# Moving the first output products and the value quarters in the attention stage of a decoder trunk

## The chip, the cores and the metric

The kernel runs on one core of a Trainium2 chip. The metric is the device time of one execution in microseconds, the median of several runs. Engines are named as in the profile: PE is TensorE (matmuls), PEld its weight loads, DVE is VectorE, ACT is ScalarE, POOL is GpSimd, SP is the engine that issues the DMAs.

## What is computed

A trunk of two layers on 512 tokens of width 1024: a layer with a pooling mixer and a layer with stick-breaking attention (16 heads of 64), each followed by a squared-ReLU MLP of width 4096, with RMSNorms before and after each part. The change lies in the attention layer. Its core, cut from the reference:

```python
for i in range(S // Q_BLOCK):
    kv_len = (i + 1) * Q_BLOCK
    ...
    z = jnp.einsum('bhqd,bhkd->bhqk', q_blk, k_blk) * inv_sqrt_d
    mask = s_idx < t_idx
    log1m = jnp.where(mask, -jax.nn.softplus(z), 0.0)
    excl = lax.cumsum(log1m, axis=3, reverse=True) - log1m
    a = jnp.where(mask, jnp.exp(jax.nn.log_sigmoid(z) + excl), 0.0)
    outs.append(jnp.einsum('bhqk,bhkd->bhqd', a, v_blk))
...
q = jnp.matmul(h, w_q[j])
k, v = jnp.split(jnp.matmul(rms_norm(x, kv_norm_g), w_kv), 2, -1)
m = jnp.matmul(o, w_o[j])
```

## The kernel before

All matmuls run at high precision: each operand is split into a rounded part ("hi") and the remainder ("lo"), and a product is three matmuls, hi·hi, hi·lo, lo·hi (`mm3`, and `up_block` for the projections). The split of a weight is a copy on ACT (line 170) and a subtraction on DVE (line 172). Most attention weights are split during the MLP of layer 0, where `split_apart` takes them from the list `apart` and writes both parts to DRAM (`kept`); in the attention stage they come back by two DMAs each (line 243). Two are not in that list, o0 and o1, the first two blocks of the output projection: they are loaded raw (line 160) and split when their turn comes.

The attention stage works on eight pairs of heads. TensorE's order is written out in `ATT_ORDER` and is kept as written (`manual_schedule`); the orders of ACT, DVE and SP within the stage are found by the scheduler, with constraints such as `issue_after`. A word of the list is a letter, a pair (or a group of values) and its parts:

- `H`, `N`: the values of the first 8 heads, in halves, with the last norms of layer 0 between them.
- `P` k and q projections of a pair (48 matmuls, lines 719 to 723), `K` the first part of a k projection, `J` its rest, `Q` the q projection alone. Each result is split by ACT and DVE (lines 966 and 967).
- `S` scores of a pair (`scores`, line 1082, six PSUM banks), followed on ACT and DVE by sigmoids (1005, 1017), the scan (1021) and the product that gives the weights (1027), for two heads.
- `T` transposes of a pair's weights (`turn`, line 1040, six banks, 20 matmuls), copied out as `ah` by ACT (1046) and `al` by DVE (1050).
- `A` attention products of a pair (line 1057), copied out by ACT and DVE (1064, 1068) and split (292, 293) into a tile `ohl`, of which there are five.
- `V2s`, `V3s`: quarter s (128 tokens) of the values of heads 8 to 11 and 12 to 15 (24 matmuls of 256 columns, lines 311 to 313), written to one of two value tiles by ACT and DVE (898, 899). `V2` is used by pairs 4 and 5, `V3` by pairs 6 and 7. The first two value tiles are in the same two buffers, and serve pairs 0, 1 and 2, 3.
- `O0`, with two blocks of tokens at a time: the output products of pairs 0 and 1 (`out_proj`, `contract`; 24 matmuls of 512 columns), copied to `y` by ACT (line 456).
- `E`: `end()`, which does pair 7's scores and all other output products in `END_ORDER`.

PSUM has eight tiles, taken in turn (line 112). Weights are asked for in the order of their first use (`want`, lines 262 to 277), and loaded ahead by `fill`, up to four at a time, which runs after each projection, each `S`, and each block of tokens in `contract`. They take four buffers in turn (three `w`, one `wx`, `place`), so each waits for the release of the weight four places earlier. A raw weight needs one of the two `raw` buffers besides. `weight` puts the ACT and DVE halves of a split behind the latest such instructions at the time of the `fill` (`behind`).

The list of weights to be split in the MLP is the list of attention weights in their order of use, without o0 and o1, with the two parts v02, v03 moved behind q1 (lines 278 to 282).

Of the kernel before, what the change touches and what calls it, by code (L numbers as in the profile page):

```python
# [57 lines left out]

ATT_ORDER = [
    (w[0], int(w[1]), [int(c) for c in w[2:]])  # L60
    for w in """H001 N2 H101 N3 H023 H123 P0 K12 S0 P1 T0 K23 S1 J2 A0 Q2 T1 K33 S2 J3 A1 Q3 O001 T2 O023 S3 A2 P4 V20 T3 V21
    S4 A3 P5 V22 T4 V23 S5 A4 P6 V30 T5 V31 S6 A5 V323 P7 T6 E1""".split()
]

# [35 lines left out]
def trunk(ctx, tc, x, consts, grow, pw, wup, wdn, wq, wk, wv, wo, out):  # L106
# [68 lines left out]
    def gains(lo, n):  # L175


        def scaled(raw):
            m = max(n, 4)
            for k in range(m):  # L180
                c, at = raw[:, k * D // m : (k + 1) * D // m], lo + k * n // m
                nc.scalar.mul(c, c, gc[:, at : at + 1])  # L182

        return scaled

    gate, queue, made, ahead, dn_pool, att_pool, dn_raw = [False], [], {}, 4, [None], [None], {}

    def want(key, src, scaled=None):
        queue.append((key, src, scaled))
# [16 lines left out]
    apart, kept, going = [], {}, []  # L206
# [52 lines left out]
    for l in range(2):  # L259
        if l == 1:  # L260
            n = len(queue)
            for what, i, part in ATT_ORDER:
                if what == "H" and not i and 0 in part:
                    for h in range(4):
                        want(("v", 0, h), wv[h], gains(C_KV * KC + 2 * h, 2))
                elif what == "V" and 0 in part:
                    for h in range(2):
                        want(("v", i, h), wv[2 * i + h], gains(C_KV * KC + 4 * h, 4))
                elif what == "K":
                    want(("k", i), wk[i], gains(C_KV * KC, KC))  # L270
                elif what in "PQ":
                    if ("k", i) not in [k for k, _, _ in queue]:
                        want(("k", i), wk[i], gains(C_KV * KC, KC))
                    want(("q", i), wq[i], gains(C_MIX_PRE1 * KC, KC))
                elif what == "O" and 0 in part or what == "E":
                    for c in range(2 * i, 2 * i + 2 if what == "O" else PAIRS):
                        want(("o", c), wo[c])
            apart.extend(x for x in queue[n:] if x[0] not in [("o", c) for c in range(2)])
            at = [k for k, _, _ in apart].index(("v", 0, 2))
            later = [apart.pop(at) for _ in range(2)]  # L280
            at = [k for k, _, _ in apart].index(("q", 1)) + 1
            apart[at:at] = later

            queue[n - GRP : n + GRP] = queue[n : n + GRP] + queue[n - GRP : n]
        for j in range(NJ):
            want(("up", l, j), wup[l, j])
        for j in range(NJ - GRP, NJ):
            want(("dn", l, j), wdn[l, j])
# [442 lines left out]
    with tc.tile_pool(name="mix0", bufs=1, reuse_waits="tile") as mp:  # L731
# [12 lines left out]
        at = P + 4 * KC  # L744
# [145 lines left out]
    with tc.tile_pool(name="att", bufs=1, reuse_waits="tile") as ap:  # L890
# [82 lines left out]
        with tc.issue_after(latest["pool"].ins):  # L973
            nc.gpsimd.memset(begin, 0.0)
            for lo, n in SEG.values():
                c = min(n - P, 1)
# [371 lines left out]
```

## Time and profile before

| | |
|---|---|
| median of 3 runs | 948.79 us (948.14 to 948.91) |
| the profiled execution | 948.49 us, of which the span of the trace is 946.7 us |
| granted TensorE clock, mean | 0.999 |
| attention stage, first scores to the first of pair 7's | 403.9 to 561.4 us of the span |

Times of rows are microseconds from the start of the span. A row of the timeline gives the start, the length from the first start to the last end of a merged group, engine, line, operation, output and inputs (the program's names, without their numbers), sizes, and the count; behind it in brackets the idle time of the engine before it and what ended that. A row of the waits gives who waited for whom, the total in us, how often, and the longest. Ends of matmuls are modelled and neighbours overlap, so steps are measured from start to start.

### The profile page before, as it was taken

How to read it: one execution, taken by the hardware profiler on the slowest of the kernel's cores; microseconds unless marked ns; L12 is line 12 of the kernel's file. 1: busy time of each engine (PE TensorE's matmuls, PEld its weight loads, DVE VectorE, ACT ScalarE, POOL GpSimd, SP SyncE). 2: the span in 40 equal slices, each digit the busy share in tenths (PEclk: the TensorE clock that was granted, in tenths of full speed). 3: DMA queues.
4: the chain of work that ended last, by engine and by line, in shares of the span. 5: the costliest groups of instructions: out<-in, count | busy, mean ns of one | idle time of the engine just before them, and what ended most of it. 6: DMA issues, size and time to landing. Idle time of an engine off the chain costs nothing.

```text
span 946.7 us, 12348 instructions
## 1 busy us (share of the span) xinstructions
PE 937.5 (99%) x4701; PEld 789.6 (83%) x4702; DVE 696.2 (74%) x797; ACT 560.0 (59%) x983; POOL 41.1 (4%) x83
## 2 busy tenths in 40 slices
PE   9999999999999999999999999999999999999996
PEld 7998888888888888888888988898888888888885
DVE  5875798988978976278466668884696966958756
ACT  6667979888775647166544444875545444444532
POOL 2300000000000004000000001200000000000002
PEclk9999999999999999999999999999999999999999
DMA  8344969789697860631335271442514233133102
GB/s 312 95 178 144 345 219 347 291 282 356 218 323 266 293 203 2 222 134 45 136 109 179 98 259 45 136 154 82 184 45 142 81 133 111 45 134 112 39 6 90
DMA packets 43262, 156.15 MB, mean 165 GB/s; under 512 B 4289, under 2 KB 4673, under 8 KB 43202
## 3 DMA queue, kind: packets, MB, share of 16 engines
q1 hardware_dynamic: 43202, 155.36, 46.5%
q8 instruction: 37, 0.61, 0.3%
q14 instruction: 23, 0.19, 0.1%
HBM read 121.79 MB, written 33.55 MB: 164 GB/s over the span
## 4 chain that ended last, share of the span: by engine, by line
PE 95%; DVE 2%; ACT 1%; POOL 1%; issue 1%; POOLq 0%; DVEq 0%; ACTq 0%
PE ps L600 28%; PE ps L722 15%; PE ps L719 15%; PE ps L723 15%; PE ps L312 4%; PE ps L311 4%; PE ps L313 4%; PE ps L1057 2%; PE ps L1082 2%; PE ps L1040 2%; PE ps L840 1%; PE ps L406 1%; PE ps L812 1%; PE ps L767 1%; ACT xn L296 1%
## 5 line engine op out<-in xcount | busy, mean ns | idle before, releaser
L600 PE MATMUL ps<-w,a 128*128 128x512 f32 x1176 | 278.6, 389 | 0.0
L722 PE MATMUL ps<-xnh,w 128*128 128x512 f32 (+1 forms) x704 | 260.5, 372 | 0.0
L723 PE MATMUL ps<-xnl,w 128*128 128x512 f32 (+1 forms) x704 | 259.8, 370 | 0.0
L719 PE MATMUL ps<-xnh,w 128*128 128x512 f32 (+1 forms) x704 | 259.2, 370 | 0.1
L600 PEld LDWEIGHTS ps<-w,a 128*128 128x128 f32 x1176 | 220.7, 188 | 45.9 <-DVE w L293 0.2
L719 PEld LDWEIGHTS ps<-xnh,w 128*128 128x128 f32 x704 | 132.1, 188 | 22.9 <-DVE w L861 0.3
L723 PEld LDWEIGHTS ps<-xnl,w 128*128 128x128 f32 x704 | 132.7, 188 | 22.1
L722 PEld LDWEIGHTS ps<-xnh,w 128*128 128x128 f32 x704 | 132.3, 188 | 22.4
L609 DVE TENSOR_TENSOR y<-ps,y 128x512 f32<-128x512 f32 x124 | 84.2, 685 | 43.6 <-PE ps L600 43.5
L172 DVE TENSOR_TENSOR w<-raw,w 128x1024 fp32r<-128x1024 f32 x58 | 70.8, 1221 | 57.8 <-ACT w L170 57.6
L170 ACT CAST w<-raw 128x1024 fp32r<-128x1024 f32 x58 | 61.1, 1053 | 80.6 <-PE ps L719 80.6
L292 ACT CAST a<-r 128x768 fp32r<-128x768 f32 (+1 forms) x60 | 47.6, 794 | 71.9 <-PE ps L600 55.4
L293 DVE TENSOR_TENSOR a<-r,a 128x768 fp32r<-128x768 f32 (+1 forms) x60 | 54.0, 900 | 11.7 <-ACT a L292 11.6
L1021 DVE TENSOR_TENSOR_SCAN e<-u,begin 128x1280 f32<-128x1280 f32 x16 | 45.2, 2825 | 19.8 <-ACT u L1005 19.0
L292 ACT CAST w<-e 128x1536 fp32r<-128x1536 f32 (+1 forms) x30 | 41.9, 1395 | 22.8 <-DVE e L574 13.4
L293 DVE TENSOR_TENSOR w<-e,w 128x1536 fp32r<-128x1536 f32 (+1 forms) x30 | 49.4, 1646 | 1.8 <-ACT w L292 1.6
L182 ACT ACTIVATE apart<-apart,eye 128x128 f32<-128x128 f32 (+1 forms) x132 | 43.1, 406 | 0.7 <-DMA apart<-in_wk 0.7
L293 DVE TENSOR_TENSOR w<-w,w 128x1536 fp32r<-128x1536 f32 (+1 forms) x20 | 33.0, 1649 | 8.2 <-ACT w L292 8.2
L632 ACT ACTIVATE r<-ps 128x512 f32<-128x512 f32 x56 | 33.0, 589 | 8.9 <-PE ps L719 8.9
L293 DVE TENSOR_TENSOR w<-xn,w 128x1536 fp32r<-128x1536 f32 (+1 forms) x20 | 33.0, 1650 | 5.6 <-ACT w L292 5.5
L633 ACT ACTIVATE r<-r 128x512 f32<-128x512 f32 x56 | 35.5, 633 | 1.3
L296 ACT ACTIVATE xn<-y 128x512 f32<-128x512 f32 (+1 forms) x25 | 15.3, 613 | 31.6 <-DVE y L478 27.9
(134 smaller groups left out, 1331.2 us busy)
## 6 DMA issues: line engine op xcount, KB each, us to landing
raw<-in_wup SPq DMA_DIRECT2D x64, 512.0 KB, 4.1
w<-kept SPq DMA_DIRECT2D x60, 512.0 KB, 4.3
kept<-wx SPq DMA_DIRECT2D x30, 512.0 KB, 4.5
w<-in_wdn SPq DMA_DIRECT2D x8, 1536.0 KB, 6.7
kept<-apart SPq DMA_DIRECT2D x24, 512.0 KB, 6.0
xn<-in_wdn SPq DMA_DIRECT2D x8, 1536.0 KB, 7.8
apart<-in_wk SPq DMA_DIRECT2D x7, 512.0 KB, 7.4
apart<-in_wq SPq DMA_DIRECT2D x7, 512.0 KB, 9.1
```

Source lines behind the costliest of these rows:

```text
L170: nc.scalar.copy(hi, raw)
L172: nc.vector.tensor_tensor(out=lo, in0=raw, in1=hi.bitcast(F32), op=ALU.subtract)
L182: nc.scalar.mul(c, c, gc[:, at : at + 1])
L292: latest["act"] = nc.scalar.copy(hi, src)
L293: latest["dve"] = nc.vector.tensor_tensor(out=lo, in0=src, in1=hi.bitcast(F32), op=ALU.subtract)
L311: nc.tensor.matmul(dst, ah, bh, start=start, stop=False)
L600: nc.tensor.matmul(bank, a[:, x, q, TS[t]], w[:, z, q], start=start and q == 0 and k == 0, stop=q == self.n - 1 and k == 2, skip_group_che ...
L609: nc.vector.tensor_tensor(out=part, in0=bank, in1=part, op=ALU.add)
L719: nc.tensor.matmul(pu[:, cols], wl[:, k, :], xnh[:, k, cols], start=False, stop=k == KC - 1)
L722: nc.tensor.matmul(pu[:, cols], wh[:, k, :], xnh[:, k, cols], start=k == 0, stop=False)
L723: nc.tensor.matmul(pu[:, cols], wh[:, k, :], xnl[:, k, cols], start=False, stop=False)
L1021: nc.vector.tensor_tensor_scan(out=self.e[:, ::-1], data0=self.u[:, 1:][:, ::-1], data1=begin[:, ::-1], initial=0.0, op0=ALU.mult, op1=ALU ...
```

## The change

TensorE's order from pair 3's q projection on. `O001` and `O023` move from around the transposes of pair 2 to around those of pair 5, behind pair 6's projections; the quarters of the values take the places in front: `V20`, `V21` around pair 2's transposes, `V22`, `V23` around pair 3's, `V30`, `V31` around pair 4's, and `V323` between pair 4's attention products and pair 6's projections. The order in which weights are asked for follows: v20 and v21 now stand before k4, v30 and v31 before k6, o0 and o1 between q6 and k7. The list of weights to be split is written out as `SPLIT_ORDER` instead of being derived from the order of use; the sequence it lists is the one that the lines removed from it gave in the kernel before.

```diff
 ATT_ORDER = [
     (w[0], int(w[1]), [int(c) for c in w[2:]])
-    for w in """H001 N2 H101 N3 H023 H123 P0 K12 S0 P1 T0 K23 S1 J2 A0 Q2 T1 K33 S2 J3 A1 Q3 O001 T2 O023 S3 A2 P4 V20 T3 V21
-    S4 A3 P5 V22 T4 V23 S5 A4 P6 V30 T5 V31 S6 A5 V323 P7 T6 E1""".split()
+    for w in """H001 N2 H101 N3 H023 H123 P0 K12 S0 P1 T0 K23 S1 J2 A0 Q2 T1 K33 S2 J3 A1 Q3 V20 T2 V21 S3 A2 P4 V22 T3
+    V23 S4 A3 P5 V30 T4 V31 S5 A4 V323 P6 O001 T5 O023 S6 A5 P7 T6 E1""".split()
 ]
...
+SPLIT_ORDER = """v00 v01 k0 q0 k1 q1 v02 v03 k2 q2 k3 q3 k4 q4 v20 v21 k5 q5 k6 q6 v30 v31 k7 q7
+    o2 o3 o4 o5 o6 o7""".split()
...
-            apart.extend(x for x in queue[n:] if x[0] not in [("o", c) for c in range(2)])
-            at = [k for k, _, _ in apart].index(("v", 0, 2))
-            later = [apart.pop(at) for _ in range(2)]
-            at = [k for k, _, _ in apart].index(("q", 1)) + 1
-            apart[at:at] = later
+            asked = {x[0]: x for x in queue[n:]}
+            for what in SPLIT_ORDER:
+                key = (what[0], *(int(c) for c in what[1:]))
+                apart.append(asked.pop(key))
+            assert sorted(asked) == [("o", 0), ("o", 1)]
```

## The prediction

> **What bounds the kernel now.** I read the page first, for the engine that sets the end; then the waits of TensorE; then the timeline of TensorE, ScalarE and VectorE over the attention stage, the only stage whose order changes.
>
> ```profile
> span 946.7 us, 12348 instructions
> PE 937.5 (99%) x4701; PEld 789.6 (83%) x4702; DVE 696.2 (74%) x797; ACT 560.0 (59%) x983; POOL 41.1 (4%) x83
> PE 95%; DVE 2%; ACT 1%; POOL 1%; issue 1%; POOLq 0%; DVEq 0%; ACTq 0%
> ```
>
> TensorE is busy 99% of the span and is 95% of the chain that ended last. The change adds and removes no matmul, so it can gain only where TensorE stands still, and lose only by making it stand still somewhere new. The longest of its waits from 390 to 600 us, which hold the attention stage, is this (us in total, times, longest):
>
> ```profile
> PE ps L1082 <- DVE al L1050: 0.4, 2, 0.2
> ```
>
> It is a scores step (line 1082) that waits for VectorE to empty the transposes' banks (line 1050). The timeline shows which one; the scores of pair 1 come first, then those of pair 2.
>
> ```profile
> 420.02 0.53 PE L1082 MATMUL ps<-kh,qh 64*128 64x512 f32 x2
> 421.34 0.32 PE L1082 MATMUL ps<-kh,qh 64*128 64x256 f32 x2
> 422.11 0.50 PE L722 MATMUL ps<-xnh,w 128*128 128x512 f32 x1
> ...
> 438.04 0.49 PE L1082 MATMUL ps<-kh,qh 64*128 64x512 f32 x1
> 440.85 0.38 PE L1082 MATMUL ps<-kh,qh 64*128 64x256 f32 x1 [0.22 <-DVE al L1050]
> 441.69 0.50 PE L722 MATMUL ps<-xnh,w 128*128 128x512 f32 x1
> ```
>
> From the first matmul of the scores to the first of the next projection pair 1 takes 422.11 - 420.02 = 2.09 us, pair 2 441.69 - 438.04 = 3.65 us. The same 24 matmuls lose 1.56 us there. That is the one stall in this stage worth a tenth of a per cent.
>
> **Why it stalls.** There are eight banks. Scores take six, the transposes before them six, and one block of the next keys lies between. So the second bank of the scores waits for VectorE's first `al` of these transposes, and the last two, at 440.85, for its fourth and fifth. VectorE and ScalarE around the transposes of pair 0 (first row of each block) and of pair 1 (the others):
>
> ```profile
> 417.08 3.13 DVE L1050 TENSOR_TENSOR al<-ps,ah 128x512 fp32r<-128x512 f32 x6
> ...
> 430.10 1.20 DVE L172 TENSOR_TENSOR w<-raw,w 128x1024 fp32r<-128x1024 f32 x1
> 435.90 0.69 DVE L967 TENSOR_TENSOR ql<-ps,qh 128x512 fp32r<-128x512 f32 x1
> 436.85 1.23 DVE L172 TENSOR_TENSOR w<-raw,w 128x1024 fp32r<-128x1024 f32 x1 [0.26 <-ACT w L170]
> 437.99 2.21 DVE L1050 TENSOR_TENSOR al<-ps,ah 128x512 fp32r<-128x512 f32 x4
> ```
>
> ```profile
> 416.33 2.62 ACT L1046 CAST ah<-ps 128x512 fp32r<-128x512 f32 x6
> ...
> 435.28 0.58 ACT L966 CAST qh<-ps 128x512 fp32r<-128x512 f32 x1
> 435.76 1.05 ACT L170 CAST w<-raw 128x1024 fp32r<-128x1024 f32 x1
> 436.71 2.60 ACT L1046 CAST ah<-ps 128x512 fp32r<-128x512 f32 x6
> ```
>
> The rows of lines 170 and 172 are the splits of the two output weights o0 and o1, the only ones of this stage that come raw and are split here. That of o1 stands between the queries' split and `ah`/`al`, on both engines.
>
> **What the change removes there.** The output products move behind pair 6's projections, and o0 and o1 with them; v20 and v21 take their places in the ring of weights and come already split, by DMA alone. Without o1, `ah` starts at 435.76. In the pair 0 rows `al` follows `ah` by 417.08 - 416.33 = 0.75 us, so `al` starts near 436.51 (the `ql` before it is through by then, at 435.90 plus about 0.6), 1.48 us earlier. The last banks of the scores came free 440.85 - 437.99 = 2.86 us after `al` began, so now at 439.37. Undisturbed they are wanted 421.34 - 420.02 = 1.32 us after the start, at 439.36. So o1 alone takes the stall away to within a hundredth or so; that o0's 1.20 us at 430.10 goes too moves the work ahead of it up by about another microsecond, and is the spare. Bounds for the gain: 1.56 us, the whole stall, and 0.4 us, what the waits view adds up. I take 1.56.
>
> The two differ because the view counts idle time between a matmul's end and the next start, and I count from start to start. The page "Perfetto Trace Analysis" of the Trainium skill, section "Tensor Engine Instruction (MATMUL, LD_WEIGHTS)", says that the profiler computes a matmul's end from its size and does not observe it. By that rule the starts are the measurement and the sum is 1.56; by the view's rows it would be 0.4. The trace agrees with the rule: the next projection is late by all of the 1.56 us.
>
> **What it moves, and the cover left.** The same steps stand in another order, and the kinds of neighbours stay: an output half or a value quarter on either side of the transposes.
>
> ```profile
> 453.25 0.40 PE L311 MATMUL ps<-w,ohl 128*128 128x512 f32 x1
> 458.95 1.25 PE L1040 MATMUL ps<-eye,w 128*128 128x128 f32 x10
> 461.05 0.48 PE L311 MATMUL ps<-w,ohl 128*128 128x512 f32 x1
> 466.83 0.50 PE L1082 MATMUL ps<-kh,qh 64*128 64x512 f32 x2
> ...
> 482.46 0.28 PE L311 MATMUL ps<-w,xnh 128*128 128x256 f32 x1
> 485.33 2.35 PE L1040 MATMUL ps<-eye,w 128*128 128x128 f32 x20
> 490.47 0.50 PE L1082 MATMUL ps<-kh,qh 64*128 64x512 f32 x2
> ...
> 537.76 0.50 PE L1082 MATMUL ps<-kh,qh 64*128 64x512 f32 x2
> 542.43 0.34 PE L311 MATMUL ps<-w,xnh 128*128 128x256 f32 x1
> 548.24 0.40 PE L722 MATMUL ps<-xnh,w 128*128 128x512 f32 x1
> 559.15 1.04 PE L1040 MATMUL ps<-eye,w 128*128 128x128 f32 x8
> ```
>
> The first half of the output products takes 458.95 - 453.25 = 5.70 us, the second 5.78, transposes 2.10, a quarter of values 2.87, two quarters 548.24 - 542.43 = 5.81, scores with the attention products after them 542.43 - 537.76 = 4.67, a pair's projections 10.91. Two places lose cover between scores and transposes, where ScalarE and VectorE make the weights of two heads:
>
> ```profile
> 501.94 1.49 DVE L1027 TENSOR_TENSOR w<-w,e 128x1280 f32<-128x1280 f32 x1
> ```
>
> From the scores of pair 4 at 490.47 to the end of this, the last product of its weights, are 12.96 us. Pair 2's transposes stood at 458.95; with a quarter for a half, and the stall gone, they stand at 458.95 - 5.70 + 2.87 - 1.56 = 454.56, which is 16.5 us after its scores: 3.5 us to spare. Pair 6 loses the two quarters: from 559.15 - 537.76 = 21.4 us to 15.6, which leaves 2.6. If that cover failed, every microsecond that VectorE is late would be one on TensorE. Cost of both: nothing. After pair 2's transposes only a quarter stands before the scores, as at 490.47 for pair 4, which shows no wait.
>
> The value weights v20, v21 now stand where o0, o1 did, as four loads instead of two: their buffers (those of k2 and q2) come free before the scores of pair 2 at 438.04, and the first quarter stands at 454.56 - 2.87 = 451.7. The keys and queries of pair 5 now come into the value weights' buffers, as pair 6's did, behind the same steps and with the same 4.67 us:
>
> ```profile
> 512.79 2.23 SPq L243 DMA_DIRECT2D w<-kept  x4
> ...
> 518.78 0.45 PE L722 MATMUL ps<-xnh,w 128*128 128x512 f32 x1
> ```
>
> They were issued from 512.79 for a projection that starts at 518.78, and no wait shows. The same loads one pair earlier cost nothing again. So does the load of the gain row, now behind o2's on SP's queue, which waits for the end of the second output half near 542 us: its first use comes after pair 7's scores, over 20 us later. The values of pairs 4 to 7 overwrite buffers that pairs 0 to 3 have read by then (A1 and A3 stand ahead of V20 and V30).
>
> The splits of o0 and o1 go to a place with room. Counted back from the transposes of pair 6 at 559.15 - 1.56 = 557.59: its projections' partner P7 starts at 546.7, S6 at 542.0, the second output half at 536.2, T5 at 534.1, the first half at 528.4, P6 at 517.5. The buffers of o0 and o1 (those of v30, v31) come free at 517.5; o1 is queued behind the split of k6, whose product ends at about 523.0, so it is ready by 523.0 + 0.2 + 0.58 (that split) + 1.05 + 1.23 = 526.1, and wanted at 528.4. They hide under P6. Bounds: 0 and, if they slip behind the queries' split too (5.5 us later), 531.6 - 528.4 = 3.2 us. I take 0, as nothing holds them.
>
> **Sum.** 948.49 us for the profiled execution, less 1.56, is 946.93; this execution lay 0.30 under the median of 948.79, so the median comes to 947.23. Forecast 947.2.
>
> **Rivals.** (a) *The splits come too late.* This is the way to slower. For: o1's raw load is asked for next to k7's and q7's, and SP issues in order; if it is put behind q7's, whose buffer P6 holds until 528.4, it lands late.
>
> ```profile
> 343.68 5.30 SPq L160 DMA_DIRECT2D raw<-in_wo  x2
> DMA to landing us min/median/max: 3.5/4.1/4.3
> ```
>
> Issued at 528.8, landed at 532.9, split at 535.2: TensorE stands still for about 6 us from 529, less 1.56 gained, and the time is near 953.2. It decides once the raw load is issued later than about 524.3 (529.1 + 1.56 - 2.28 - 4.1). Against: both raw loads went out at 343.68, some 80 us before their splits, since nothing but the raw buffers holds them, and that stays so. The granted clock is whole in all 40 slices, so no row shows what a stop does to it:
>
> ```profile
> PEclk9999999999999999999999999999999999999999
> ```
> The page "TensorE: Matmul & The Clock Gate", section "Part 1: The HAM clock gate", says that an idle window of about 3.4 us halves the clock until another busy one; by it this case would cost up to 1.7 us more, an estimate from that page.
>
> (b) *Only the waits view's 0.4 us comes back*, because the planner puts other work in o1's place or the scores are held by something else: 948.4. For: the view's own sum. Against: no row between `qh` and `ah` but o1's.
>
> (c) *The later small waits go too*: with the value quarters gone from behind pair 6's scores, VectorE enters the end earlier.
>
> ```profile
> 560.02 0.69 DVE L967 TENSOR_TENSOR ql<-ps,qh 128x512 fp32r<-128x512 f32 x1 [4.75 <-ACT qh L966]
> 561.42 0.45 PE L1082 MATMUL ps<-kh,qh 64*128 64x384 f32 x2
> 563.72 0.49 PE L1057 MATMUL ps<-ah,v 128*128 128x512 f32 x1
> 592.55 1.27 PE L406 MATMUL ps<-eye,xn 128*128 128x128 f32 x8 [0.16 <-ACT xn L396]
> ```
>
> Pair 6's transposes last 2.27 us (559.15 to 561.42) against 2.10, pair 7's scores 2.30 against 2.09, and the wait at 592.55 is 0.16: together 0.5, so 946.7, and 946.0 if as much again lies hidden between starts. Against: VectorE already idles for 4.75 us before that `ql`, so it enters the end no earlier.
>
> **How the numbers follow.** Forecast 0.60, (a) 0.13, (b) 0.10, (c) 0.17. The forecast's own range is 946.7 to 947.7; the range reaches over (c) and (b), 946.0 to 949.0, and leaves out most of (a). A change under 0.2%, 1.9 us, can hardly be told from none in this kernel, whose three runs spread over 0.77 us. The forecast's 0.16% lies close under that bound: I give a quarter or so of it, and all of (c), to faster by over 0.2%: 0.17 + 0.15, rounded up to 0.33; (a) is slower, 0.13; the rest, 0.54, is within 0.2%.
>
> **What would show it.** In the profile after: the scores of pair 2 near 2.1 us long and no wait for line 1050; line 172 in the attention stage near 518 to 526 us, not 430 and 437; transposes of pairs 2 and 6 without a wait before them; scores of pair 7 at 559.9. A wait of TensorE at the first output half, or before pair 6's transposes, would make the forecast wrong, as would splits that still stand between `qh` and `ah`.

## The result, and the profile after

The changed kernel takes 947.25 us (median of 20 runs, 946.57 to 947.83), the kernel before 948.64 us in the 20 runs beside it: a ratio of 0.9985, 95% interval 0.9978 to 0.9992. The forecast was 947.2 us. The profiled execution took 947.41 us, its span 945.6.

The profile's page of the changed kernel: TensorE as busy as before, and the chain that ended last now hardly leaves it (97% after 95%, VectorE 1% after 2%).

```profile
span 945.6 us, 12346 instructions
PE 936.8 (99%) x4702; PEld 789.7 (84%) x4702; DVE 696.3 (74%) x797; ACT 560.0 (59%) x983; POOL 41.1 (4%) x83
PE 97%; POOL 1%; ACT 1%; DVE 1%; issue 0%; POOLq 0%; DVEq 0%; ACTq 0%
```

All waits of TensorE in it (us in total, times, longest). The changed file has six lines more above these places, so a scores matmul is now line 1088, `al` 1056, a weight's split 176 and 178. No scores matmul waits any more.

```profile
PE ps L773 <- POOL warm L739: 1.3, 1, 1.3
PE ps L412 <- ACT xn L402: 0.2, 1, 0.2
```

The timeline of TensorE in the changed kernel, at the scores of pair 2, then at the start of pair 2's transposes, of the first output half, and of pair 6's transposes and pair 7's scores:

```profile
438.50 0.50 PE L1088 MATMUL ps<-kh,qh 64*128 64x512 f32 x2
440.56 0.50 PE L728 MATMUL ps<-xnh,w 128*128 128x512 f32 x1
...
455.03 2.35 PE L1046 MATMUL ps<-eye,w 128*128 128x128 f32 x20
...
528.84 0.40 PE L317 MATMUL ps<-w,ohl 128*128 128x512 f32 x1
...
557.96 2.24 PE L1046 MATMUL ps<-eye,w 128*128 128x128 f32 x19
560.23 0.45 PE L1088 MATMUL ps<-kh,qh 64*128 64x384 f32 x2
562.54 0.50 PE L1063 MATMUL ps<-ah,v 128*128 128x512 f32 x1
```

The scores of pair 2 last 440.56 - 438.50 = 2.06 us where they lasted 3.65, and the matmuls of the two heads go side by side again (`x2` in the row of the scores, two of them in 0.50 us; before, a single one of this size took 0.49). VectorE and ScalarE of the changed kernel show why: `ah` and `al` follow the queries' split directly, and the splits of o0 and o1 stand at 520.67 and 525.23.

```profile
435.20 0.69 DVE L973 TENSOR_TENSOR ql<-ps,qh 128x512 fp32r<-128x512 f32 x1
435.81 3.14 DVE L1056 TENSOR_TENSOR al<-ps,ah 128x512 fp32r<-128x512 f32 x6
...
520.67 1.22 DVE L178 TENSOR_TENSOR w<-raw,w 128x1024 fp32r<-128x1024 f32 x1
525.23 1.23 DVE L178 TENSOR_TENSOR w<-raw,w 128x1024 fp32r<-128x1024 f32 x1 [0.26 <-ACT w L176]
```

```profile
434.59 0.59 ACT L972 CAST qh<-ps 128x512 fp32r<-128x512 f32 x1
435.07 2.62 ACT L1052 CAST ah<-ps 128x512 fp32r<-128x512 f32 x6
```

From the first scores of pair 2 (438.04 before, 438.50 after) to pair 7's scores (561.42, 560.23) the stage became 1.65 us shorter; the 3.65 - 2.06 = 1.59 us of pair 2 are nearly all of it. The changed execution came 0.46 us later to that point. That is the spread of executions: the kernel of experiment e5 below, the same up to there, came to it at 438.0.

### The profile page after: what moved, and what is told of

The parts are those of the page before. It is cut to its first block, busy times and chain, and to the rows that moved or that the text cites. A ratio compares the mean times of both kernels' runs of the same rounds, so it can differ in the third digit from the quotient of the medians.

```text
span 945.6 us, 12346 instructions
## 1 busy us (share of the span) xinstructions
PE 936.8 (99%) x4702; PEld 789.7 (84%) x4702; DVE 696.3 (74%) x797; ACT 560.0 (59%) x983; POOL 41.1 (4%) x83
## 4 chain that ended last, share of the span: by engine, by line
PE 97%; POOL 1%; ACT 1%; DVE 1%; issue 0%; POOLq 0%; DVEq 0%; ACTq 0%
PE ps L606 28%; PE ps L728 15%; PE ps L725 15%; PE ps L729 15%; PE ps L317 4%; PE ps L318 4%; PE ps L319 4%; PE ps L1063 2%; PE ps L1046 2%; PE ps L1088 2%; PE ps L846 1%; PE ps L412 1%; PE ps L818 1%; PE ps L773 1%; ACT xn L302 1%; DVE x L368 0%
## 5 line engine op out<-in xcount | busy, mean ns | idle before, releaser
L299 DVE TENSOR_TENSOR a<-r,a 128x768 fp32r<-128x768 f32 (+1 forms) x60 | 54.1, 902 | 11.9 <-ACT a L298 11.6
```

Source lines behind the costliest of these rows:

```text
L299: latest["dve"] = nc.vector.tensor_tensor(out=lo, in0=src, in1=hi.bitcast(F32), op=ALU.subtract)
```

## The experiments

The theory: the splits of o0 and o1, above all o1's between the queries' split and `ah`/`al`, made `al` late, and pair 2's scores waited for their banks. The rival: it is the order itself, a value quarter in place of an output half around pair 2's transposes. Its loads and its ACT and DVE work differ, so this too could have freed the scores. TensorE's own order, though, is the same in both kernels up to pair 2's scores and beyond (to `Q3`), so all that can differ there is what is loaded ahead and what ScalarE and VectorE do.

**e1: old order, o1 split in the MLP of layer 0.**

```diff
-            apart.extend(x for x in queue[n:] if x[0] not in [("o", c) for c in range(2)])
+            apart.extend(x for x in queue[n:] if x[0] != ("o", 0))
+            apart.append(apart.pop([k for k, _, _ in apart].index(("o", 1))))
...
-            n = len(apart) % 5
+            n = (len(apart) - 1) % 5
...
-        steps = [n for n in range(1, 34)] if l == 0 else []
+        steps = [n for n in range(1, 35)] if l == 0 else []
```

> The old order of steps, with o1 added at the end of the list of weights that are split in the MLP of layer 0, so that it comes by two loads and only o0 is still split in the attention stage. Theory (the split of o1 stands between the queries' split and ah/al, and holds the banks of pair 2's scores): scores of pair 2 take 2.1 us instead of 3.65, no wait of line 1082, time 1.5 us below the kernel before (ratio 0.9984). Rival (it is the order: output halves around pair 2's transposes, or too little between pair 1's transposes and pair 2's scores): the scores stay at 3.65 us, ratio 1.000. The split costs about 2.3 us of ScalarE and VectorE in the MLP stage, which TensorE should not see.

Measured: 952.35 us, 1.0037 of the kernel before (1.0024 to 1.0049), so slower, and yet the scores did what the theory said. TensorE's timeline at pair 2's scores in e1 (lines stand one lower in its file):

```profile
443.39 0.50 PE L1083 MATMUL ps<-kh,qh 64*128 64x512 f32 x2
...
445.54 0.50 PE L723 MATMUL ps<-xnh,w 128*128 128x512 f32 x1
```

They last 2.15 us. The loss is elsewhere, in the end of the MLP of layer 0, among the waits of TensorE from 200 to 410 us; with them TensorE's timeline there, SP's, and windows of the trace (stretch, length, busy time of PE, PEld, DVE, ACT and POOL, granted clock, DMA share, GB/s):

```profile
PE ps L312 <- ACT dn L170: 2.2, 1, 2.2
PE ps L313 <- DVE dn L172: 0.8, 1, 0.8
```

```profile
348.71 0.39 PE L314 MATMUL ps<-dn,sq 128*128 128x512 f32 x1
351.32 0.50 PE L312 MATMUL ps<-dn,sq 128*128 128x512 f32 x1 [2.23 <-ACT dn L170]
352.58 0.79 PE L313 MATMUL ps<-dn,sq 128*128 128x512 f32 x1 [0.76 <-DVE dn L172]
```

```profile
339.92 0.32 SPq L213 DMA_DIRECT2D kept<-wx  x1
342.29 0.32 SPq L213 DMA_DIRECT2D kept<-apart  x1
342.71 1.20 SPq L243 DMA_DIRECT2D w<-kept  x2
344.02 0.45 SPq L160 DMA_DIRECT2D raw<-in_wdn  x1
```

```profile
352.00:354.00 2.00, 1.42 (x3) 1.16 (x4) 0.69 (x2) 0.00 (x0) 0.00 (x0) 0.58 0.03 10
354.00:356.00 2.00, 2.00 (x7) 1.54 (x6) 1.41 (x3) 0.82 (x3) 0.00 (x0) 0.57 0.00 0
```

The last load of a raw down weight (`in_wdn`) goes out at 344.02, behind the two writes of o1's parts and two loads of another weight, which in the kernel before had gone out by 335.3; there it went out at 341.95. It also takes longer: the copy that waits for it starts 6.2 us after it (350.22) and not 4.4. So the split is late, TensorE waits 3 us, and for about 3 us from then on it has little more than half its clock. My expectation that TensorE would not see a split in the MLP was wrong; that this load is what made TensorE late is read from the rows and was not tried by itself.

**e2: old order, only the request for o1 held back until pair 2's scores** (and, as requests go in order, those behind it with it).

```diff
-            if queue and len(made) < ahead and (queue[0][0][0] != "dn" or dn_pool[0]):
+            if queue and len(made) < ahead and not (queue[0][0] == ("o", 1) and hold[0]) and (queue[0][0][0] != "dn" or dn_pool[0]):
...
                 heads[i] = weights(i)
+                hold[0] = i < 2
```

> The old order of steps; only the request for o1 is held back until pair 2's scores, which puts its split on ScalarE and VectorE behind the six ah/al of pair 1's transposes. Theory: scores of pair 2 take 2.1 us, time 1.5 us below the kernel before (ratio 0.9984), as in the changed kernel, though no output product and no value quarter has moved. Rival (the order): 3.65 us, ratio 1.000.

Measured: 946.95 us, 0.9981 (0.9972 to 0.9990). TensorE and VectorE of e2:

```profile
438.93 0.50 PE L1082 MATMUL ps<-kh,qh 64*128 64x512 f32 x2
...
441.09 0.50 PE L722 MATMUL ps<-xnh,w 128*128 128x512 f32 x1
```

```profile
436.79 0.69 DVE L967 TENSOR_TENSOR ql<-ps,qh 128x512 fp32r<-128x512 f32 x1
437.40 3.13 DVE L1050 TENSOR_TENSOR al<-ps,ah 128x512 fp32r<-128x512 f32 x6
440.45 1.21 DVE L172 TENSOR_TENSOR w<-raw,w 128x1024 fp32r<-128x1024 f32 x1
```

The split of o1 stands behind `al` and the scores take 2.16 us. No product and no value quarter has moved, and the gain is that of the changed kernel within the intervals. The rival falls.

**e3 and e4: the changed kernel, with one and with two pairs of instructions of a split's size put back where o1's split stood** (they add work that nothing reads).

```diff
+        def split_like(n):
+            for c in range(0, 2 * n, 2):
+                with tc.issue_after(latest["act"].ins):
+                    latest["act"] = nc.scalar.copy(xn3[:, c], xt[0])
+                with tc.issue_after(latest["dve"].ins):
+                    latest["dve"] = nc.vector.tensor_tensor(out=xn3[:, 1], in0=xt[0], in1=xn3[:, c], op=ALU.subtract)
...
                 queries_keys(i, {"P": "kq", "J": "k", "Q": "q"}[what])
+                if what == "Q" and i == 2:
+                    split_like(1)
```

> The changed kernel, with one copy on ScalarE and one subtraction on VectorE of 128 x 1024 that nobody reads, put where o1's split stood (behind the queries' split of pair 2, ahead of ah/al). Theory: al starts 1.4 us later than in the changed kernel (its first bank free at 3.2 us after the start of the transposes, the last needed at 5.7 and free at 6.05), so the scores of pair 2 take 2.1 + 0.4 = 2.5 us; time 0.4 us above the changed kernel, ratio to the kernel before 0.999. Rival (the order): 2.1 us, no change against the changed kernel.

> The changed kernel with two such pairs of instructions in the same place. Theory: al another 1.15 us later, scores of pair 2 take 2.1 + 1.6 = 3.7 us, so the time comes back to that of the kernel before, ratio 1.000. Rival (the order): 2.1 us, ratio 0.9985.

Measured: e3 947.83 us, 0.9990 (0.9982 to 0.9999); e4 949.01 us, 1.0001 (0.9992 to 1.0010). TensorE at the transposes of pair 1 and the scores of pair 2, in e3:

```profile
434.34 2.35 PE L1046 MATMUL ps<-eye,w 128*128 128x128 f32 x20
438.70 0.50 PE L1088 MATMUL ps<-kh,qh 64*128 64x512 f32 x2
...
441.22 0.50 PE L728 MATMUL ps<-xnh,w 128*128 128x512 f32 x1
```

and in e4:

```profile
434.02 2.35 PE L1046 MATMUL ps<-eye,w 128*128 128x128 f32 x20
438.38 0.49 PE L1088 MATMUL ps<-kh,qh 64*128 64x512 f32 x1
...
441.39 0.38 PE L1088 MATMUL ps<-kh,qh 64*128 64x256 f32 x1 [0.21 <-DVE al L1056]
...
442.23 0.50 PE L728 MATMUL ps<-xnh,w 128*128 128x512 f32 x1
```

VectorE's `al` between them, first in e3, then in e4:

```profile
437.52 3.14 DVE L1056 TENSOR_TENSOR al<-ps,ah 128x512 fp32r<-128x512 f32 x6
...
438.53 3.14 DVE L1056 TENSOR_TENSOR al<-ps,ah 128x512 fp32r<-128x512 f32 x6
```

The scores take 2.52 and 3.85 us, where 2.5 and 3.7 were expected. Nothing, one and two splits in that place cost 0, 0.46 and 1.79 us: two bring the old time back under the new order. The first costs only a third of its length because `al` has about a microsecond to spare, and the second, which moves `al` by 1.33 us, is paid in full. Side by side, from the start of pair 1's transposes to that of `al`, and from the first matmul of pair 2's scores to the next projection, in us:

| | changed | e1 | e2 | e3 | before | e4 |
|---|---|---|---|---|---|---|
| `al` starts after | 1.68 | 2.84 | 2.84 | 3.18 | 4.32 | 4.51 |
| scores of pair 2 | 2.06 | 2.15 | 2.16 | 2.52 | 3.65 | 3.85 |

Up to 2.84 us the scores hardly notice; from there to 4.51, 1.67 us more for `al` are 1.69 us more for the scores, whatever the order of the steps. In e3 the waits of TensorE list no scores matmul at all; the 0.46 us are seen only from start to start.

**e5 and e6: the changed kernel with two and with five subtractions more on VectorE between the weights of pair 6's two heads** (again work that nothing reads), for the cover before pair 6's transposes.

```diff
+                    late = nullcontext()
+                    if p == 6 and x.a:
+                        for _ in range(2):
+                            d = nc.vector.tensor_tensor(out=xn3[:, 1], in0=hs[0].w[:, :D], in1=xt[0], op=ALU.subtract)
+                        late = tc.issue_after(d.ins)
+                    with late:
-                    x.scan()
+                        x.scan()
```

> The changed kernel, with two subtractions of 128 x 1024 that nobody reads on VectorE between the weights of the two heads of pair 6 (2.3 us). They test the cover before pair 6's transposes, which the change cut from 21.4 to 15.6 us. Theory (2.6 us to spare for the first head's ten transposes, whose weights are not delayed, and 3.7 for the second head's, which are): no wait, time as the changed kernel. Rival (the cover is already used up): pair 6's transposes wait about 2 us.

> The same with five such subtractions (5.7 us), behind which the planner also leaves a split of 1.2 us ahead of the second head's weights. Theory: the second head's transposes wait 12.96 + 5.7 + 1.2 - 16.6 = 3.2 us, and the time is 3 us above the changed kernel (950.3, ratio to the kernel before 1.0017). Rival (VectorE's lateness is hidden elsewhere): no change.

Measured: e5 947.18 us, 0.9984 (0.9974 to 0.9994), no wait before pair 6's transposes; e6 951.63 us, 1.0031 (1.0019 to 1.0043). TensorE in e6, at the ten transposes of each head, and its windows:

```profile
557.67 1.25 PE L1046 MATMUL ps<-eye,w 128*128 128x128 f32 x10
562.11 1.61 PE L1046 MATMUL ps<-eye,w 128*128 128x128 f32 x10 [3.18 <-DVE w L1033]
563.65 0.69 PE L1088 MATMUL ps<-kh,qh 64*128 64x384 f32 x2
...
566.91 0.50 PE L1063 MATMUL ps<-ah,v 128*128 128x512 f32 x1
```

```profile
561.00:563.00 2.00, 0.89 (x8) 0.93 (x9) 2.00 (x3) 0.17 (x1) 0.00 (x0) 0.98 0.37 152
563.00:565.00 2.00, 2.00 (x12) 1.67 (x12) 2.00 (x5) 1.24 (x3) 0.00 (x0) 0.50 0.03 8
```

The wait is 3.18 us, 3.2 was expected, so the reckoning of the cover holds at both points: the 2.3 us of e5 cost nothing, and what e6 adds beyond the cover is paid. The time rose by 4.4 us over the changed kernel's and not by 3, in the main because the clock is 0.50 from 563 us on: pair 7's scores take 566.91 - 563.65 = 3.26 us instead of 562.54 - 560.23 = 2.31.

**e7: the changed kernel with o1's raw load held back** until pair 6's queries are split, the prediction's rival (a) made to happen (`hold` as in e2, lifted at pair 6's queries, and a dependency of the load on that split).

```diff
+        load = nc.sync.dma_start(raw, src)
+        if behind_of is not None:
+            info = mybir.DependencyInfo(mybir.DependencyClass.Sync, mybir.DependencyReason.DATA)
+            tc.add_manual_dep(load.ins, behind_of.ins.name, info, reason="late")
...
+                hold[0] = (p, what) != (6, "q")
                 fill()
```

> The changed kernel, with the raw load of o1 held until the queries' split of pair 6 is done (near 529.7 us), so behind the loads for pair 7's keys. It prices the prediction's rival (a). Theory: landed 4.1 us later, split by 536, wanted at 529.5: TensorE waits 6 to 6.5 us at the first output half; time 953.5, ratio to the kernel before 1.005. If the clock of TensorE falls after so long a wait, up to 1.7 us more. Rival (other work fills the wait): under 2 us.

Measured: 958.83 us, 1.0107 (1.0091 to 1.0122), about twice the expected loss. SP, ScalarE and TensorE of e7, and its windows:

```profile
528.87 0.80 SPq L252 DMA_DIRECT2D w<-kept  x2
529.71 0.43 SPq L155 DMA_DIRECT2D grow<-in_grow  x1
530.27 0.34 SPq L166 DMA_DIRECT2D raw<-in_wo  x1
```

```profile
536.64 1.04 ACT L179 CAST w<-raw 128x1024 fp32r<-128x1024 f32 x1 [7.12 <-DMA raw<-in_wo]
```

```profile
529.14 0.40 PE L322 MATMUL ps<-w,ohl 128*128 128x512 f32 x1
537.73 0.79 PE L320 MATMUL ps<-w,ohl 128*128 128x512 f32 x1 [8.20 <-ACT w L179]
539.00 0.80 PE L321 MATMUL ps<-w,ohl 128*128 128x512 f32 x1 [0.47 <-DVE w L181]
```

```profile
540.00:542.00 2.00, 2.00 (x6) 1.61 (x5) 0.00 (x0) 0.59 (x1) 0.00 (x0) 0.50 0.00 0
544.00:546.10 2.10, 2.10 (x10) 1.65 (x9) 0.00 (x0) 0.59 (x1) 0.00 (x0) 0.94 0.04 8
```

The load went out at 530.27, right behind two weight parts and the gain row, and the copy started 6.4 us later, not 4.1; that the three loads ahead of it made it slow is likely but was not tried by itself. TensorE waited 8.2 us, and then ran its products at half the clock until about 544. The mechanism of the rival is real; the changed kernel has none of it, since there the raw loads have gone out by 349 us.

## Why the prediction was right

- *How near it came.* That 947.2 met 947.25 is in part luck. The forecast was counted down from a median of 948.79, and beside the changed kernel the one before measured 948.64. The gain is 1.39 us by these medians, 0.8 to 2.1 by the interval; that leaves out the 0.4 us of rival (b), but it is the timeline that tells 1.56 from 1.39.
- *The stall and its size.* 1.56 us were read from start to start where the waits view had 0.4. The scores became 1.59 us shorter; of the two readings that the prediction weighed, the one by starts was right. The page "Perfetto Trace Analysis" of the Trainium skill, section "Tensor Engine Instruction (MATMUL, LD_WEIGHTS)", on modelled ends, agrees with e3, where 0.46 us do not show as a wait. Rival (b) is out.
- *Its cause.* "o1 alone takes the stall away, o0 is the spare": e2 moved o1 alone and left 2.16 us, 0.1 above undisturbed, where the prediction had a hundredth or so. `al` then started 2.84 us after the transposes (437.40 - 434.56), which is what the prediction's 436.51 comes to (436.51 - 433.67). The converse was not in the prediction but follows from it: o1's place costs only 0.46 us if nothing stands ahead (e3). So neither split is the cause alone; the two together are, each eating the spare that the other needs. No run parted o1's copy on ScalarE from its subtraction on VectorE; by the rows it was the subtraction that held `al`, which started at 437.99, about as that ended and 1.28 us after `ah`, not 0.75 as for pair 0.
- *The new places.* With the 0.46 us by which this execution came later taken off, the starts that the prediction gave for pair 2's transposes, the first output half, pair 6's transposes and pair 7's scores (454.56, 528.4, 557.59, 559.9) stand beside 454.57, 528.38, 557.50 and 559.77. The split of o1 ended at 525.23 + 1.23 - 0.46 = 526.0, where 526.1 was forecast. No wait came up at any of these places, and e5 and e6 bear out the spare time that was reckoned before pair 6's transposes.
- *Rival (c), the end gains too.* It did not: pair 6's transposes still take 2.27 us, pair 7's scores 2.31, and the wait of 0.2 us is there as before.
- *Rival (a)* did not come about. The prediction read both raw loads as issued at 343.68; that is the first of the two, the second went out at 348.7, still some 80 us before its split. The rival's price was set too low: e7 cost 11.6 us more than the changed kernel (958.83 - 947.25), where the prediction had about 6 us of waiting and up to 1.7 more as an estimate for the clock. The landing was mis-sized (4.1 us for some 6.4), the half clock lasted longer than was allowed for, and 1.5 us are e7's own, whose load went out at 530.27 where the prediction's example had 528.8.

## What to carry to other kernels

When one engine is busy all the time, look in its timeline for a step that takes longer than its like, start to start; the list of waits showed a quarter of the 1.56 us here and nothing of e3's 0.46. Work that is "off the critical path" costs by its place in the queue: here the same split was free behind the instructions that release the banks (e2), cost 0.46 us ahead of them (e3), and its whole length where a second stood there too (e4). And before a large reordering, try moving the small thing alone: holding back one request made pair 2's scores 1.49 us shorter, moving nine steps 1.59.

## What the runs showed that I had not expected

TensorE's clock fell behind waits of a few microseconds. In e1 one wait of 2.2 us, with one matmul and a second wait of 0.8 us behind it, brought it to 0.50 from about 352.3 to 355.7 us; in e6 3.18 us brought it to 0.50 from about 563 to 566; in e7 8.2 us did, until about 6 us after the end of the wait. The stalls of pair 2's scores, 1.6 to 1.8 us in all with matmuls between, did not: there the clock is 1.00 in every microsecond, before and in e4.

These waits, too, are longer from start to start: TensorE was held up by 3.4 us in e1, 3.4 in e6 and 9.4 in e7, and lost another 1.6, 1.3 and 2.5 us behind that, mostly at half clock. So in these three runs the slow clock cost a quarter to a half of the wait again. The sums, 5.0, 4.7 and 11.9 us, account for what the medians show: e1 lost 5.1 us (952.35 - 948.74 + 1.5), e6 4.4, e7 11.6. Where between 1.8 us in pieces and 2.2 and 0.8 us in a row the clock begins to fall, no run shows.

The page "TensorE: Matmul & The Clock Gate" of the Trainium skill, section "Part 1: The HAM clock gate", puts the idle window at about 3.4 us. The trace of e6 agrees, with about 3.5 us from start to start. In e1 neither gap is that long (2.6 and 1.3 us from start to start, one matmul between); whether the two count as one, no run here shows.
